# Rotating the queries of both head groups of a token tile in one set of vector operations, inside the loaded buffer

## The chip, the cores and the metric

The kernel runs on one core of a Trainium2 chip. The metric is the device time of one execution in microseconds (us): the median of three runs of the kernel before is 1649.61 us (1648.79 to 1650.91). Beside the times there is one profiled execution, with a record of each instruction on the engines: PE (TensorE, matmuls and transposes into PSUM), DVE (VectorE), ACT (ScalarE), POOL (GpSimd, unused here) and SP, whose queue issues all the DMAs.

## The reference

The kernel computes one encoder block on 1024 tokens of width 1024, in float32. A normalised input is projected into the inputs of two branches. Branch A is gated linear attention, branch B is softmax attention in a window of 128 tokens to both sides, with 8 query heads in 2 groups of 4 that share a key and value head. The branches are gated, summed and projected, and a SwiGLU feed-forward block follows. The part that matters here is the query side of branch B:

```python
q = _rope(_rms_norm(q.reshape(bsz, s, SWA_HEADS, hd), q_g), pos)
...
scores = jnp.einsum("bnqhgd,bnkhd->bnhgqk", qb, kc) * (hd ** -0.5)
...
m = jnp.maximum(scores.max(axis=-1, keepdims=True), sink)
p = jnp.exp(scores - m)
```

with `_rope` turning the two halves of a head's 128 values: `[x1*cos - x2*sin, x2*cos + x1*sin]`.

## The kernel before

Matmul operands are split into a high and a low part (`ACTIVATE Copy` on ACT writes the high part, a subtraction on DVE the low part), and a product is three matmuls. So nearly every matmul operand costs one ACT and one DVE instruction.

The program has these stages in time: the input and first projections; linear attention of branch A, with dense projections between its steps; softmax attention of branch B, with dense projections between its steps (about 384 to 578 us in the profile); the rest of the gate projections; output projections; and the feed-forward block.

Branch B works on 8 tiles of 128 tokens (t = 0 to 7) and 2 groups of heads (g = 0, 1). The list `todo` (L796 to L809) puts the steps of a tile and group into slots; a slot is one turn of a loop, and each step is a function that emits instructions:

- `prep(t)`, slot 2t+1: loads the 8 heads of queries of a tile from DRAM into `qr` (two DMAs, L665, buffer of 128 x 1024 values, two buffers), squares them on ACT (L666), loads keys and values of the next tile (L671), squares the keys (L672), sums the squares of each head on DVE (L674), takes an inverse root (L96 to L101) into `rs`, and rotates the next tile's keys (`rope_k`, L646 to L654).
- `a_rope(g, t)`, slot 2t+1 for g = 0 and 2t+2 for g = 1: four DVE operations on the 4 heads of a group. Two products with the sine table write the halves of `rq` (L699, L701), one with the cosine table writes a new tile `qn4` (L703), and a sum adds `rq` to it in place (L704). The query norm's gain is in the tables `qA` and `qB`; the inverse root `rs` is applied later, in the softmax.
- `a_turn(g, t)`, slot 2t+2+g: PE transposes the 4 heads (L710), ACT and DVE split them (L713, L714).
- `a_scores(g, t, h)`, four times, slot 2t+3+g: scores of a head (L727, through the helper `mm` at L73), added to the band and reduced to a maximum on DVE (L728); after the fourth head the softmax: small DVE operations, four exponentials (L743) and four scalings (L749) on ACT.
- `a_probs(g, t, kb)`, up to three times, slot 2t+4+g: PE transposes the probabilities of a block of keys (L760), ACT and DVE split them (`ph` at L763, `pl` at L764).
- `a_out(g, t)`, slot 2t+5+g: products with the values, copied by ACT (L774) and stored by four DMAs (L776).
- `k_turn(t)`, transposes of keys (L689), in even slots.

In a slot the steps are sorted by `order` (L810), and `slot` (L273) runs them one after the other and spreads a fixed number of dense matmuls evenly behind them (`share(SF, t)`: 24 in slots 2 to 8, 18 in slots 9 to 17). These dense matmuls (L245 and L73 with an `mm` bank) belong to the projections; their results go out by DVE (L248) and DMA (L251), and their weights are split by L67 and L69. Scores, transposes, probabilities and outputs share four PSUM banks (`ch`); a bank comes free when ACT or DVE has read it.

PE runs in the order in which the code is written (`manual_schedule`). The order of DVE's, ACT's and SP's instructions is chosen at build time by the framework's planner, from priorities in the order of the program and estimated times; on the chip each of these queues then runs strictly in that order, and waits at its head hold everything behind them. A buffer of a pool is handed on when all that read it are done.

Of the kernel before, what the change touches and what calls it, by code (L numbers as in the profile page):

```python
# [8 lines left out]
F32 = mybir.dt.float32  # L9
# [3 lines left out]
ALU = mybir.AluOpType  # L13

P = 128
# [15 lines left out]
def body(tc, i, out):  # L31
    nc = tc.nc
    with ExitStack() as root:
# [8 lines left out]
        def nm(s):  # L42
            uid[0] += 1
            return f"{s}_{uid[0]}"
# [49 lines left out]
        def rsqrt(dst, v, scale, epsv, eps_t, pool, shape, tag):  # L94
            l = pool.tile(list(shape), F32, tag=tag + "l", name=nm("rl"))
            nc.scalar.activation(l, v, AF.Ln, bias=eps_t[:, 0:1], scale=scale)  # L96
            nc.scalar.activation(l, l, AF.Exp, scale=-0.5)
            t = pool.tile(list(shape), F32, tag=tag + "t", name=nm("rt"))
            nc.vector.scalar_tensor_tensor(t, l, -0.5 * scale, l, op0=ALU.mult, op1=ALU.mult)
            nc.vector.scalar_tensor_tensor(t, v, epsv / scale, t, op0=ALU.add, op1=ALU.mult)  # L100
            nc.vector.scalar_tensor_tensor(dst, t, 1.5, l, op0=ALU.add, op1=ALU.mult)  # L101
# [167 lines left out]
        def need(key):  # L269
            while key not in scr:  # L270
                fill(12)
# [346 lines left out]
        sw = swas.enter_context(tc.tile_pool(name="swt", bufs=2))  # L618
# [7 lines left out]
        qA = sc_.tile([P, KT, P], F32, tag="qA", name="qA")  # L626
        qB = sc_.tile([P, KT, P], F32, tag="qB", name="qB")
# [12 lines left out]
        keys, att = {}, {}  # L640

        def rope_k(raw, rs, t):
            qn = sw.tile([P, 2, P], F32, tag="qn2", name=nm("qn"))
            b = sw.tile([P, 2, P], F32, tag="sq2", name=nm("sq"))
            for h in range(2):
                nc.vector.scalar_tensor_tensor(qn[:, h], raw[:, h], rs[:, h:h + 1], kg, op0=ALU.mult, op1=ALU.mult)  # L646
            c = cosb[:, t:t + 1].to_broadcast([P, 2, 64])
            s = sinb[:, t:t + 1].to_broadcast([P, 2, 64])
            nc.vector.tensor_tensor(b[:, :, 0:64], qn[:, :, 64:128], s, op=ALU.mult)
            nc.vector.tensor_tensor(b[:, :, 64:128], qn[:, :, 0:64], s, op=ALU.mult)  # L650
            nc.vector.tensor_tensor(qn[:, :, 0:64], qn[:, :, 0:64], c, op=ALU.mult)
            nc.vector.tensor_tensor(qn[:, :, 64:128], qn[:, :, 64:128], c, op=ALU.mult)
            nc.vector.tensor_tensor(qn[:, :, 0:64], qn[:, :, 0:64], b[:, :, 0:64], op=ALU.subtract)
            nc.vector.tensor_tensor(qn[:, :, 64:128], qn[:, :, 64:128], b[:, :, 64:128], op=ALU.add)  # L654
            return qn

        def prep(t):
            sq = sw.tile([P, 10, P], F32, tag="sq", name=nm("sq"), bufs=1)
            lo, hi = 8, 8
            if t >= 0:  # L660
                lo = 0
                qr = sw.tile([P, 8, P], F32, tag="qr", name=nm("qr"))
                for g in range(2):
                    need((f"sq{g}", t))
                    nc.sync.dma_start(out=qr[:, 4 * g:4 * g + 4].rearrange("p a b -> p (a b)"), in_=scr[f"sq{g}", t])  # L665
                nc.scalar.activation(sq[:, 0:8], qr, AF.Square)  # L666
            if t + 1 < KT:
                hi = 10
                kv = sw.tile([P, 4, P], F32, tag="kvr", name=nm("kvr"), bufs=1)
                need(("skv", t + 1))  # L670
                nc.sync.dma_start(out=kv.rearrange("p a b -> p (a b)"), in_=scr["skv", t + 1])  # L671
                nc.scalar.activation(sq[:, 8:10], kv[:, 0:2], AF.Square)  # L672
            ss = sw.tile([P, 10], F32, tag="ss", name=nm("ss"))
            nc.vector.tensor_reduce(ss[:, lo:hi], sq[:, lo:hi], axis=mybir.AxisListType.X, op=ALU.add)  # L674
            rs = sw.tile([P, 10], F32, tag="rs", name=nm("rs"), bufs=4)
            rsqrt(rs[:, lo:hi], ss[:, lo:hi], 1.0, EPS * 128, eps128, sw, (P, hi - lo), f"sn{hi - lo}")
            if t + 1 < KT:
                keys[t + 1] = rope_k(kv, rs[:, 8:10], t + 1)
                v2 = kv[:, 2:4].rearrange("p a b -> p (a b)")
                nc.scalar.activation(vSh[t + 1], v2, AF.Copy)  # L680
                nc.vector.tensor_tensor(vSl[t + 1], v2, vSh[t + 1].bitcast(F32), op=ALU.subtract)
            for g in range(2 if t >= 0 else 0):
                a = att[g, t] = Chunk()
                a.qr, a.rs = qr[:, 4 * g:4 * g + 4], rs[:, 4 * g:4 * g + 4]

        def k_turn(t):
            kt = chtile((P, 2, P))
# [3 lines left out]
            nc.scalar.activation(kTh[:, :, c], kt, AF.Copy)  # L691
            nc.vector.tensor_tensor(kTl[:, :, c], kt, kTh[:, :, c].bitcast(F32), op=ALU.subtract)

        def a_rope(g, n):
            a = att[g, n]
            qr = a.qr
            b = sw.tile([P, 4, P], F32, tag="rq", name=nm("rq"), bufs=1)
            a.qn = sw.tile([P, 4, P], F32, tag="qn4", name=nm("qn"))
            nc.vector.tensor_tensor(b[:, :, 0:64], qr[:, :, 64:128], qB[:, n:n + 1, 0:64].to_broadcast([P, 4, 64]),  # L699
                                    op=ALU.mult)  # L700
            nc.vector.tensor_tensor(b[:, :, 64:128], qr[:, :, 0:64], qB[:, n:n + 1, 64:128].to_broadcast([P, 4, 64]),  # L701
                                    op=ALU.mult)
            nc.vector.tensor_tensor(a.qn, qr, qA[:, n:n + 1].to_broadcast([P, 4, P]), op=ALU.mult)  # L703
            nc.vector.tensor_tensor(a.qn, a.qn, b, op=ALU.add)  # L704

        def a_turn(g, n):
            a = att[g, n]
# [87 lines left out]

        todo = [[] for _ in range(2 * KT + 6)]  # L796
        todo[0].append((prep, -1))
        todo[1].append((k_turn, 0))
        for n in range(2 * KT):
            t, g = divmod(n, 2)  # L800
            todo[n + 5].append((a_out, g, t))
            todo[n + 4] += [(a_probs, g, t, kb) for kb in range(3)]
            todo[n + 3] += [(a_scores, g, t, h) for h in range(4)]
            todo[n + 2].append((a_turn, g, t))
            todo[n + 1].append((a_rope, g, t))
            if g == 0:
                todo[n + 1].append((prep, t))
                if t + 1 < KT:
                    todo[n + 2].append((k_turn, t + 1))  # L809
        order = (prep, a_rope, a_scores, a_turn, k_turn, a_out, a_probs)  # L810
        with tc.manual_schedule(engines={mybir.EngineType.PE}):
            for t, v in enumerate(todo):
# [229 lines left out]
        def gate(nme, s):  # L1042
            g = bt.tile([P, HT], F32, tag=nme[:2], name=nm(nme[:2]))
            nc.sync.dma_start(out=g, in_=scr[nme, s])
            nc.scalar.activation(g, g, AF.Sigmoid)
            return g
# [119 lines left out]
        with tc.manual_schedule(engines={mybir.EngineType.PE}):  # L1166
# [29 lines left out]
            for m in (0, 4, 1, 5, 2, 6, 3, 7):  # L1196
                g = [gate(f"gb{m}", s) for s in range(2)]
# [345 lines left out]
```

## Time and profile before

| what | value |
|---|---|
| median of three runs | 1649.61 us |
| the profiled execution's own time | 1647.86 us |
| its span, first to last instruction | 1646.1 us |
| mean granted TensorE clock | 0.995 |
| PE busy | 1621.1 us (98%), 7644 matmuls and transposes |
| DVE busy | 1230.9 us (75%), 2358 instructions |
| ACT busy | 913.7 us (56%), 1867 instructions |
| `qr` loads (L665) | 16 |
| rotation of queries (L699, L701, L703, L704) | 16 instructions a line |

A line of the trace that begins with two numbers gives the start and the duration of an instruction in us, then engine, line of the kernel, operation, output and inputs by the program's names with the buffer numbers left out, and in square brackets the idle time of the engine before it and what ended it. A line of waits gives who waited for whom, the total in us, how many times, and the longest. Busy time is the share in which an engine ran anything; idle time of an engine that nobody waits for costs nothing.

### The profile page before, as it was taken

The numbers are of one execution on the slowest core, as the hardware profiler recorded it, in microseconds if no ns is written. First come the engines' busy times: TensorE is split into PE (matmuls) and PEld (weight loads), VectorE is DVE, ScalarE is ACT, GpSimd is POOL, SyncE is SP. The second block draws the span as 40 slices with busy tenths as digits, with TensorE's granted clock in tenths as the row PEclk, the third lists the DMA queues.
The fourth block names the chain that finished last, engine by engine and source line by source line (L and its number), as shares of the span: only waits on it lengthen the run. The fifth ranks groups of instructions, "written<-read, shape, count | busy, mean of one in ns | idle before, by whom it ended". The sixth has DMA issues, their size and how long they took to land.

```text
span 1646.1 us, 23402 instructions
## 1 busy us (share of the span) xinstructions
PE 1621.1 (98%) x7644; PEld 1346.5 (82%) x7644; DVE 1230.9 (75%) x2358; ACT 913.7 (56%) x1867; POOL 0.2 (0%) x4
## 2 busy tenths in 40 slices
PE   9999999999999999998999999999999999999999
PEld 7888888888888788886888888888888888788887
DVE  8568787846999677785865787776767787779655
ACT  7456776863988745453633546754444444354442
POOL 0000000000000000000000000000000000000000
PEclk9999999999999999998999999999999999999999
DMA  8856757778543387776842476643444555595433
GB/s 284 292 167 205 240 186 241 268 265 298 188 133 116 123 288 248 250 230 229 262 131 89 143 228 201 202 152 129 130 127 150 196 191 174 185 335 190 148 99 118
DMA packets 195787, 322.21 MB, mean 196 GB/s; under 512 B 22254, under 2 KB 47726, under 8 KB 195664
## 3 DMA queue, kind: packets, MB, share of 16 engines
q1 hardware_dynamic: 195664, 320.71, 59.4%
q8 instruction: 60, 0.98, 0.3%
q14 instruction: 63, 0.52, 0.1%
HBM read 215.24 MB, written 105.38 MB: 195 GB/s over the span
## 4 chain that ended last, share of the span: by engine, by line
PE 88%; DVE 5%; ACT 4%; DMA 2%; issue 1%; SPq 0%; ACTq 0%; DVEq 0%
PE mm L73 19%; PE mm L852 10%; PE mm L854 10%; PE mm L853 10%; PE mm L1383 7%; PE ch L73 7%; PE ch L1383 5%; PE ch L852 5%; PE ch L854 5%; PE ch L853 5%; PE mm L245 3%; PE ch L760 1%; ACT p L743 1%; DVE G L421 1%; DVE wl L69 0%
## 5 line engine op out<-in xcount | busy, mean ns | idle before, releaser
L831 ACT ACTIVATE wh<-ws 128x512 fp32r<-128x512 f32 x164 | 103.2, 630 | 155.2 <-PE mm L853 87.4
L73 PE MATMUL mm<-wh,xh 128*128 128x512 f32 x320 | 127.3, 398 | 0.1
L73 PE MATMUL mm<-wh,xl 128*128 128x512 f32 x320 | 127.1, 397 | 0.0
L73 PE MATMUL mm<-wl,xh 128*128 128x512 f32 x320 | 126.6, 396 | 0.0
L832 DVE TENSOR_TENSOR wl<-ws,wh 128x512 fp32r<-128x512 f32 x164 | 112.4, 686 | 15.8 <-ACT wh L831 15.1
L67 ACT ACTIVATE wh<-wr 128x512 fp32r<-128x512 f32 x118 | 73.8, 627 | 59.6 <-PE mm L73 25.8
L69 DVE TENSOR_TENSOR wl<-wr,wh 128x512 fp32r<-128x512 f32 x118 | 81.0, 688 | 22.6 <-ACT wh L67 20.0
L831 ACT ACTIVATE wh<-a 128x512 fp32r<-128x512 f32 x66 | 41.7, 632 | 91.0 <-PE ch L1383 42.3
L831 ACT ACTIVATE wh<-wr 128x512 fp32r<-128x512 f32 x72 | 45.4, 631 | 55.7 <-PE mm L853 16.9
L832 DVE TENSOR_TENSOR wl<-a,wh 128x512 fp32r<-128x512 f32 x66 | 45.6, 692 | 40.5 <-ACT wh L831 40.2
L1383 PE MATMUL mm<-hh,wh 128*128 128x512 f32 x176 | 68.6, 390 | 0.5 <-DVE c L1322 0.5
L1383 PE MATMUL mm<-hl,wh 128*128 128x512 f32 x176 | 68.6, 390 | 0.0
L1383 PE MATMUL mm<-hh,wl 128*128 128x512 f32 x176 | 68.5, 389 | 0.0
L73 PEld LDWEIGHTS mm<-wl,xh 128*128 128x128 f32 x320 | 60.2, 188 | 9.9
L73 PEld LDWEIGHTS mm<-wh,xl 128*128 128x128 f32 x320 | 60.2, 188 | 9.7
L73 PEld LDWEIGHTS mm<-wh,xh 128*128 128x128 f32 x320 | 60.2, 188 | 9.3 <-ACT st L220 0.3
L845 DVE TENSOR_TENSOR ws<-wr,wr 128x512 f32<-128x512 f32 x80 | 54.8, 688 | 6.3 <-DMA wr<-in_w_f_dram 3.6
L1356 DVE TENSOR_TENSOR hl<-hr,hh 128x512 fp32r<-128x512 f32 x77 | 52.9, 687 | 5.9 <-ACT hh L1355 5.7
L832 DVE TENSOR_TENSOR wl<-wr,wh 128x512 fp32r<-128x512 f32 x72 | 49.3, 686 | 5.6 <-ACT wh L831 4.7
L1355 ACT ACTIVATE hh<-hr 128x512 fp32r<-128x512 f32 x77 | 47.6, 619 | 8.8 <-DMA hr<-B 4.9
L1383 PE MATMUL ch<-hh,wh 128*128 128x512 f32 x132 | 51.3, 389 | 0.0
L1383 PE MATMUL ch<-hl,wh 128*128 128x512 f32 x132 | 51.3, 389 | 0.0
(453 smaller groups left out, 5008.4 us busy)
## 6 DMA issues: line engine op xcount, KB each, us to landing
wr<-in_w_fi_dram SPq DMA_DIRECT2D x110, 256.0 KB, 3.9
wr<-in_w_f_dram SPq DMA_DIRECT2D x100, 256.0 KB, 3.4
wh<-wh SPq DMA_DIRECT2D x80, 256.0 KB, 2.9
wl<-wl SPq DMA_DIRECT2D x80, 256.0 KB, 2.9
B<-c SPq DMA_DIRECT2D x44, 256.0 KB, 2.1
T<-st SPq DMA_DIRECT2D x44, 256.0 KB, 2.9
a<-in_w_fo_dram SPq DMA_DIRECT2D x44, 256.0 KB, 5.2
hr<-T SPq DMA_DIRECT2D x44, 256.0 KB, 2.6
```

The costliest lines, as they stand in the source:

```text
L67: nc.scalar.activation(h, raw, AF.Copy)
L69: nc.vector.tensor_tensor(l, raw, h.bitcast(F32), op=ALU.subtract)
L73: nc.tensor.matmul(o, a, b, start=start, stop=stop)
L245: nc.tensor.matmul(Y[q], w[:, c], x, start=f0, stop=f1, skip_group_check=True)
L831: nc.scalar.activation(h, src, AF.Copy)
L832: nc.vector.tensor_tensor(l, src, h.bitcast(F32), op=ALU.subtract)
L845: nc.vector.tensor_tensor(t, x, y, op=op)
L852: nc.tensor.matmul(o, h[:, c], x[kk][0], start=start and kk == 0, stop=False, skip_group_check=True)
L853: nc.tensor.matmul(o, h[:, c], x[kk][1], start=False, stop=False, skip_group_check=True)
L854: nc.tensor.matmul(o, l[:, c], x[kk][0], start=False, stop=kk == nk - 1, skip_group_check=True)
L1356: nc.vector.tensor_tensor(l, r, h.bitcast(F32), op=ALU.subtract)
L1383: nc.tensor.matmul(ys[m], a[:, c], b, start=f0, stop=f1, skip_group_check=True)
```

## The change

`a_rope` is called once for a token tile, in slot 2t+1, in place of once for each group in slots 2t+1 and 2t+2. Its operations take all 8 heads. The product with the cosine table and the sum write into `qr` itself, so the tile `qn4` (two buffers of 2 KB a partition) is gone, and `rq` has twice its size (4 KB a partition, one buffer). `a_turn` reads its 4 heads from `qr`. Even slots have one step less; the number of dense matmuls in a slot stays.

```diff
             for g in range(2 if t >= 0 else 0):
                 a = att[g, t] = Chunk()
-                a.qr, a.rs = qr[:, 4 * g:4 * g + 4], rs[:, 4 * g:4 * g + 4]
+                a.q8, a.qn, a.rs = qr, qr[:, 4 * g:4 * g + 4], rs[:, 4 * g:4 * g + 4]
...
-        def a_rope(g, n):
-            a = att[g, n]
-            qr = a.qr
-            b = sw.tile([P, 4, P], F32, tag="rq", name=nm("rq"), bufs=1)
-            a.qn = sw.tile([P, 4, P], F32, tag="qn4", name=nm("qn"))
-            nc.vector.tensor_tensor(b[:, :, 0:64], qr[:, :, 64:128], qB[:, n:n + 1, 0:64].to_broadcast([P, 4, 64]),
-                                    op=ALU.mult)
-            nc.vector.tensor_tensor(b[:, :, 64:128], qr[:, :, 0:64], qB[:, n:n + 1, 64:128].to_broadcast([P, 4, 64]),
-                                    op=ALU.mult)
-            nc.vector.tensor_tensor(a.qn, qr, qA[:, n:n + 1].to_broadcast([P, 4, P]), op=ALU.mult)
-            nc.vector.tensor_tensor(a.qn, a.qn, b, op=ALU.add)
+        def a_rope(n):
+            qr = att[0, n].q8
+            b = sw.tile([P, 8, P], F32, tag="rq", name=nm("rq"), bufs=1)
+            for d, o in ((0, 64), (64, 0)):
+                nc.vector.tensor_tensor(b[:, :, d:d + 64], qr[:, :, o:o + 64],
+                                        qB[:, n:n + 1, d:d + 64].to_broadcast([P, 8, 64]), op=ALU.mult)
+            nc.vector.tensor_tensor(qr, qr, qA[:, n:n + 1].to_broadcast([P, 8, P]), op=ALU.mult)
+            nc.vector.tensor_tensor(qr, qr, b, op=ALU.add)
...
-            todo[n + 1].append((a_rope, g, t))
             if g == 0:
-                todo[n + 1].append((prep, t))
+                todo[n + 1] += [(a_rope, t), (prep, t)]
```

## The prediction

> **What bounds the kernel now.** I read the page's first part, then the busy times of each engine by stretch over the attention stage (its work runs from about 384 to 578 us), then who waited for whom in it.
>
> ```profile
> span 1646.1 us, 23402 instructions
> PE 1621.1 (98%) x7644; PEld 1346.5 (82%) x7644; DVE 1230.9 (75%) x2358; ACT 913.7 (56%) x1867; POOL 0.2 (0%) x4
> ```
>
> ```profile
> 400.00:560.00 160.00, 156.60 (x847) 132.47 (x846) 146.35 (x450) 139.88 (x337) 0.00 (x0) 1.00 0.48 154
> 560.00:580.00 20.00, 17.47 (x79) 13.44 (x78) 9.28 (x26) 11.54 (x28) 0.00 (x0) 0.91 0.40 116
> ```
>
> TensorE sets the time: it is idle for 25.0 us of the whole span. Columns of the second view: stretch, its length, PE, PEld, DVE, ACT, POOL, granted clock, DMA. From 400 to 560 PE idles 3.4 us, in the last 20 us another 2.5 us, and there the granted clock averages 0.91, which loses up to 0.09 x 20 = 1.8 us. So all that this stage can give is 3.4 + 2.5 + 1.8 = 7.7 us. DVE has 13.7 us free in 160 and ACT 20.1: neither is the bound of the stage, but each is full enough that the order of its queue shows.
>
> ```profile
> PE ch L73 <- DVE pl L764: 1.5, 2, 0.8
> PE ch L73 <- DVE sql L714: 0.8, 1, 0.8
> PE ch L73 <- DVE mx L728: 0.6, 3, 0.2
> PE ch L73 <- DVE rd L747: 0.4, 1, 0.4
> ACT sq L666 <- DMA qr<-sq: 3.1, 3, 1.3
> SPq L251 <- DVE st L248: 28.2, 15, 6.5
> ```
>
> (Total, times, longest, 380 to 565 us.) What DVE costs PE here is 1.5 + 0.8 + 0.6 + 0.4 = 3.3 us. No rotation (L699 to L704) is waited for by PE; it only stands in DVE's queue ahead of what is.
>
> **Fewer, longer instructions.** Per token tile four pairs become four single operations of twice the width: 64 DVE instructions in eight tiles become 32.
>
> ```profile
> 384.27 0.42 DVE L699 TENSOR_TENSOR rq<-qr,qB 128x256 f32<-128x256 f32 x1
> 384.61 0.42 DVE L701 TENSOR_TENSOR rq<-qr,qB 128x256 f32<-128x256 f32 x1
> 384.94 1.29 DVE L703 TENSOR_TENSOR qn<-qr,qA 128x512 f32<-128x512 f32 x2
> 386.15 0.69 DVE L704 TENSOR_TENSOR qn<-qn,rq 128x512 f32<-128x512 f32 x1
> ```
>
> ```profile
> L674 DVE TENSOR_REDUCE ss<-sq 128x8 f32<-128x1024 f32 x1 | 1.2, 1220 | 0.0
> ```
>
> By durations a tile costs 2 x (2 x 0.42 + 2 x 0.69) = 4.44 us now and 2 x 0.69 + 2 x 1.22 = 3.82 after; the 1.22 is the row of another operation over 1024 elements, since no such multiply is in the trace. But starts lie closer than durations: 0.34 us apart at 256 elements, (386.15 - 384.94) / 2 = 0.605 at 512, so 0.605 + 2 x (0.605 - 0.34) = 1.135 at 1024. By starts a tile costs 3.78 us now and 3.48 after: 0.30 less, 2.4 us in eight tiles. I take the starts, for back to back is how they run. The in-place product is no extra cost: L704, in place already, lasts as long as half of the L703 pair. All of it lies beside PE's work; alone it is worth nothing, except through the order below.
>
> The Trainium skill ("VectorE: DVE Perf Modes", The DRAIN you can't avoid) says that the next operation does not start until the pipe is empty, and its rules for authors ask for fewer operations. By that the whole fixed part, 2 x 0.42 - 0.69 = 0.15 us, would be saved 32 times, 4.8 us of DVE. The rows differ: L701 starts 0.08 us before L699 ends.
>
> **The second group's rotation moves a slot earlier.** Slot 2t+2 loses it (1.89 us by starts), slot 2t+1 has 3.48 us in place of 1.89. This is where the odd slot of tile 5 has its wait:
>
> ```profile
> 482.28 1.48 DVE L674 TENSOR_REDUCE ss<-sq 128x10 f32<-128x1280 f32 x1
> 484.00 0.42 DVE L699 TENSOR_TENSOR rq<-qr,qB 128x256 f32<-128x256 f32 x1
> 485.79 0.69 DVE L703 TENSOR_TENSOR qn<-qr,qA 128x512 f32<-128x512 f32 x1
> 486.47 0.69 DVE L69 TENSOR_TENSOR wl<-wr,wh 128x512 fp32r<-128x512 f32 x1
> 487.16 1.85 DVE L764 TENSOR_TENSOR pl<-ch,ph 128x512 fp32r<-128x512 f32 x3
> 488.93 0.69 DVE L704 TENSOR_TENSOR qn<-qn,rq 128x512 f32<-128x512 f32 x1
> ```
>
> ```profile
> 486.17 1.54 ACT L763 ACTIVATE ph<-ch 128x512 fp32r<-128x512 f32 x3
> ```
>
> ```profile
> 487.96 0.41 PE L73 MATMUL ch<-kTh,sqh 128*128 128x384 f32 x1 [0.80 <-DVE pl L764]
> ```
>
> PE's second score waits 0.80 us for a PSUM bank that pl (L764) frees. The first ph ends near 486.75 (1.54 us hold three), so pl could start there and started at 487.16: DVE owns 0.41 of the wait, ACT the rest. Behind the changed rotation the three operations ahead of pl grow by 2 x 0.265 + 0.53 = 1.06 us, but the slot before has given up 1.89. If the free time is used, pl starts with ph: -0.41 us a tile. If the 1.135 us product stands right ahead of pl, as a 0.6 us operation does now: +0.53. For tiles 2 to 7 that is -2.5 to +3.2 us; the ends nearly cancel and I take 0.
>
> **The loaded queries are held longer.** qr has two buffers. Now the last read of a tile is L703 of group 1; after the change the rotated queries lie in qr, so its buffer comes free when PE has transposed group 1 (L710).
>
> ```profile
> 474.69 0.69 DVE L703 TENSOR_TENSOR qn<-qr,qA 128x512 f32<-128x512 f32 x1
> 504.41 1.48 DVE L674 TENSOR_REDUCE ss<-sq 128x10 f32<-128x1280 f32 x1
> ```
>
> ```profile
> 475.40 0.32 SPq L665 DMA_DIRECT2D qr<-sq  x1
> ```
>
> ```profile
> 490.76 0.60 PE L710 MATMUL ch<-ident,qn 128*128 128x128 f32 x4
> ```
>
> ```profile
> DMA to landing us min/median/max: 2.6/3.7/5.4
> ```
>
> ```profile
> 490.44 1.06 ACT L666 ACTIVATE sq<-qr 128x1024 f32<-128x1024 f32 x1
> 494.84 1.27 ACT L763 ACTIVATE ph<-ch 128x512 fp32r<-128x512 f32 x2 [0.31 <-PE ch L760]
> 504.25 0.59 ACT L774 COPY st<-ch 128x512 f32<-128x512 f32 x1 [0.75 <-PE ch L73]
> ```
>
> The load of tile 6 goes out at 475.40, as soon as L703 is done; it would go out at about 491.4, 16 us later, and land by 495.1 (497.2 with the longest landing). Its square (L666) then ends by 498.3 at best, and the sum that needs it ran at 504.41: 6 us remain, so the wait for data costs nothing. It is the place on ACT that changes: the square ran at 490.44; after the change it comes into the stretch from 494.84 on in which ACT idles next only for 0.75 us ahead of 504.25. Its 1.06 us push what follows by up to 1.06 - 0.75 = 0.31 us, and the chain ACT, ph, pl, PE is the one just shown. Four steady tiles: 0 to +1.2 us; I take a third, +0.4, since only some slots wait there at all. On SP the two loads now wait for PE; behind them stand the stores of results and the loads of dense weights. SP stood up to 6.5 us on a dense store without a wait of PE, so that is covered; uncovered, it would be part of the first rival. The product in place also waits for ACT's square: 498.3 against a rotation that starts after the sum, no cost.
>
> **The run-ahead at the start goes.** Tiles 2 and 3 are now prepared two slots ahead, and that has a price:
>
> ```profile
> 409.24 1.49 DVE L674 TENSOR_REDUCE ss<-sq 128x10 f32<-128x1280 f32 x1 [0.28 <-ACT sq L672]
> ```
>
> ```profile
> 399.80 0.99 SPq L665 DMA_DIRECT2D qr<-sq  x2
> ```
>
> ```profile
> 408.50 0.60 PE L710 MATMUL ch<-ident,qn 128*128 128x128 f32 x4
> ...
> 411.52 0.38 PE L73 MATMUL ch<-kTh,sql 128*128 128x256 f32 x1 [0.79 <-DVE sql L714]
> ```
>
> The sum of tile 2 stands ahead of sql, for which PE waits 0.79 us. Its load went out at 399.8 and could now go only after the transposes of tile 0's second group (L710 at 408.50), so the sum comes later and this wait may go: -0.8 to 0, I take -0.4.
>
> **PE's own order.** In the eight even slots one stage is gone, so the one or two dense matmuls that stood ahead of the first score come behind it.
>
> ```profile
> 496.67 0.39 PE L245 MATMUL mm<-xh,wl 128*128 128x512 f32 x1
> 496.90 0.34 PE L73 MATMUL ch<-kTh,sqh 128*128 128x384 f32 x1
> ```
>
> The first score of an even slot has no wait in the trace, and as many dense matmuls are issued in the slot as before: 0; bound +1.8 (eight times the 0.23 us from the dense matmul's start to the next).
>
> **Sum.** 0 + 0.4 - 0.4 + 0 = 0 on the span of 1646.1 us and on the profiled execution's 1647.86, which is 1.75 below the median of the timed runs. I forecast that median, 1649.6.
>
> **Rivals.** (1) Slower: ACT stands at the square. The queue of ACT is fixed at build time; if the square is put where its data are thought to be there, and the load behind PE and SP comes later, exponentials and ph of the running tile stand behind it. Three times ACT waited for qr already, 3.1 us, 1.03 each. For tiles 2 to 7 that is 6 x 1.03 = 6.2 us if all of it passes to PE: 1655.8. It decides as soon as the landing is later than ACT's slack of 0.75 us. For it: the load is now gated by PE for six tiles. Against: 6 us to the sum. Chance 0.19.
> The Trainium skill ("Perfetto Trace Analysis", Identifying Performance Opportunities) takes a gap that repeats on the saturated engine as a sign of too few buffers. Longer use of qr's two would make one a tile; the trace of before shows 0.80 at 487.96 but behind pl, not behind a load.
> (2) Faster: the freed 2.4 us and the early wait let DVE catch up, and all 3.3 us go: 1646.3, on the edge of what can be told. Against: half of the wait shown is ACT's. Chance 0.26.
> (3) The end of the stage shifts.
>
> ```profile
> 567.97 0.50 PE L73 MATMUL ch<-ph,vSh 128*128 128x512 f32 x1 [1.31 <-ACT ph L763]
> ```
>
> There PE waits and its clock falls: 2.5 + 1.8 = 4.3 us. No rotation is left there, yet another order of DVE before it could close it, 1645.3 (0.12), or double it, 1653.9 (0.08).
>
> **How the numbers follow.** Forecast 0.35; with its own bounds (-2.5 - 0.8 to +3.2 + 1.2 + 1.8) it reaches from 1646.3 to 1655.8, most of it within 1648 to 1652. Against no change 0.2%, 3.3 us, can be told. Faster: half of (2) and the closed end, 0.13 + 0.12 = 0.25. Slower: (1) and the doubled end, 0.27. Same: 0.48. The range 1645.0 to 1656.0 takes in every case's price.
>
> **What would show it.** Right: 32 DVE instructions fewer; the wide ones at 0.69 and 1.22 us; loads of qr right behind L710's last transpose; square after 495 us without a DMA wait on ACT; PE busy from 400 to 560 within 1 us of 156.6. Wrong: ACT idle on qr in several tiles, pl waits over 1.2 us in odd slots, or another PE idle time near 565 us.

## The result and the profile after

The changed kernel takes 1664.28 us (median of 6 runs, 1660.7 to 1665.73) against 1649.2 (6 runs beside them): a ratio of 1.0087, 95% interval 1.0074 to 1.0100, some 15 us slower. The forecast was 1649.6, with a range that ended at 1656.0. The profiled execution of the changed kernel took 1664.0 us.

The lines of the changed kernel lie a few lower than before: products into `rq` L698, the two operations in place L700 and L701, the transposes of the queries L707, the score evacuation L725, `ph` L760, `pl` L761. The first two lines of its page, and then its busy times by stretch (columns as in the prediction):

```profile
span 1662.2 us, 23387 instructions
PE 1628.2 (98%) x7644; PEld 1348.2 (81%) x7644; DVE 1229.1 (74%) x2326; ACT 915.0 (55%) x1867; POOL 0.2 (0%) x4
```

```profile
400.00:560.00 160.00, 147.43 (x760) 121.63 (x759) 136.72 (x391) 126.50 (x301) 0.00 (x0) 0.98 0.47 147
400.00:600.00 200.00, 184.94 (x939) 151.26 (x938) 158.98 (x453) 153.61 (x366) 0.00 (x0) 0.97 0.45 140
460.00:480.00 20.00, 16.73 (x81) 13.86 (x80) 16.19 (x47) 15.76 (x37) 0.00 (x0) 0.91 0.36 122
500.00:520.00 20.00, 18.47 (x94) 15.21 (x93) 17.96 (x51) 13.85 (x33) 0.00 (x0) 0.91 0.40 129
```

From 400 to 560 TensorE did 760 matmuls where it had done 847; it idles 12.6 us instead of 3.4, and in two stretches the granted clock averages 0.91, which was 1.00 there before. Up to 384 us both have run the same matmuls but one (2029 and 2028). The first matmul behind the stage, in the timelines of the kernel before and of the changed one, shows that all of the loss lies inside it:

```profile
595.27 0.39 PE L852 MATMUL ch<-xh,wh 128*128 128x512 f32 x1
```

```profile
613.13 0.39 PE L848 MATMUL ch<-xh,wh 128*128 128x512 f32 x1
```

It starts 17.9 us later, and from there to the end the two spans are 1050.8 and 1049.1 us. From 384 us to this matmul PE idles 15.4 us where it idled 5.9. The other 8.4 us of the delay are time in which PE is busy but gets the same work done more slowly. The clock has a part in it: it averages 0.83 from 470 to 480 and from 510 to 520 us, 0.79 from 580 to 590 and 0.87 from 590 to 600, where the kernel before has one such stretch (0.83 from 570 to 580).

The instructions themselves came out as the prediction had them. Groups of the changed kernel from 380 to 600 us, with total and mean ns:

```profile
L698 DVE TENSOR_TENSOR rq<-qr,qB 128x512 f32<-128x512 f32 x16 | 10.5, 683 | 5.4 <-DMA qr<-sq 5.4
L701 DVE TENSOR_TENSOR qr<-qr,rq 128x1024 f32<-128x1024 f32 x8 | 9.7, 1218 | 0.0
L700 DVE TENSOR_TENSOR qr<-qr,qA 128x1024 f32<-128x1024 f32 x8 | 9.7, 1217 | 0.1
```

What changed is who waits for whom. Waits of the changed kernel from 380 to 600 us (total, times, longest):

```profile
PE ch L73 <- DVE pl L761: 3.5, 5, 1.4
PE ch L707 <- DVE mx L725: 3.3, 1, 3.3
PE ch L73 <- DVE mx L725: 3.0, 5, 0.9
PE ch L73 <- ACT ph L760: 2.1, 2, 1.3
PE ch L73 <- DVE sql L711: 0.9, 1, 0.9
ACT sq L666 <- DMA qr<-sq: 6.6, 6, 2.8
DVE rq L698 <- DMA qr<-sq: 5.4, 3, 2.7
```

Before, PE's waits that end on the score evacuation were 0.6 us; now they are 6.3. ACT's waits for the loaded queries doubled from 3.1 us, and DVE's are 5.4 where they were 4.3, but PE waits for neither directly: it waits for PSUM banks that DVE empties late. The longest of these waits, as the timeline has it on DVE, on ACT, on PE and on the queue of SP:

```profile
455.87 1.29 DVE L698 TENSOR_TENSOR rq<-qr,qB 128x512 f32<-128x512 f32 x2 [0.58 <-DMA qr<-sq]
...
467.90 0.69 DVE L248 TENSOR_TENSOR st<-mm,rstd 128x512 f32<-128x512 f32 x1 [2.03 <-DMA b<-st]
468.62 1.89 DVE L761 TENSOR_TENSOR pl<-ch,ph 128x512 fp32r<-128x512 f32 x3
470.42 0.68 DVE L69 TENSOR_TENSOR wl<-wr,wh 128x512 fp32r<-128x512 f32 x1
471.05 1.23 DVE L700 TENSOR_TENSOR qr<-qr,qA 128x1024 f32<-128x1024 f32 x1
472.20 1.48 DVE L674 TENSOR_REDUCE ss<-sq 128x10 f32<-128x1280 f32 x1
473.59 0.41 DVE L681 TENSOR_TENSOR vSl<-kvr,vSh 128x256 fp32r<-128x256 f32 x1
473.93 1.22 DVE L701 TENSOR_TENSOR qr<-qr,rq 128x1024 f32<-128x1024 f32 x1
475.16 0.55 DVE L725 CUSTOM_DVE_ANT_0 p<-ch,band 128x384 f32<-128x384 f32 x1
```

```profile
469.96 1.05 ACT L666 ACTIVATE sq<-qr 128x1024 f32<-128x1024 f32 x1
479.85 1.06 ACT L666 ACTIVATE sq<-qr 128x1024 f32<-128x1024 f32 x1 [2.79 <-DMA qr<-sq]
```

```profile
468.86 0.34 PE L73 MATMUL ch<-kTh,sqh 128*128 128x384 f32 x1
472.11 0.39 PE L245 MATMUL mm<-xl,wh 128*128 128x512 f32 x1
475.77 0.66 PE L707 MATMUL ch<-ident,qr 128*128 128x128 f32 x4 [3.27 <-DVE mx L725]
477.33 0.63 PE L73 MATMUL ch<-pl,vSh 128*128 128x512 f32 x1
```

```profile
476.46 0.80 SPq L665 DMA_DIRECT2D qr<-sq  x2
```

Read from the bottom of the wait: PE computed the four heads' scores from 468.86 on and filled all four `ch` banks. The next step needs a bank, and the first evacuation (L725) ran only at 475.16. Ahead of it DVE had stood 2.03 us behind a store, then did three `pl`, a weight split, and from 471.05 to 475.07 the rotation with the sum of squares between its halves. The products into `rq` had run at 455.87; L700 may not run before the square, at 469.96 in ACT's queue, has read what it overwrites. It starts as that ends, but DVE, busy with the weight split until then, shows no wait for it: what can be seen is where L700 stands in the queue, not that the square held it up. The wait behind the store is new as well (5.9 us in two waits from 380 to 600 us, none before), and no run takes it away alone; a later kernel without any such wait, the one with the in-place operations halved, is still 11 us slower than the kernel before. Behind the gap the matmuls of 512 columns last 0.63 us instead of 0.39. And only now, with the transposes at 475.77, is the buffer free: the next load goes out at 476.46, so the lateness goes into the next tile, whose square makes ACT wait 2.79 us.

The Trainium skill ("TensorE: Matmul & The Clock Gate", Part 1: The HAM clock gate) says that TensorE falls to half its clock after an idle window of about 3.4 us. The trace agrees in kind, with a gap a little shorter than that: the 3.27 us are followed by the 0.63 us matmuls, and the granted clock averages 0.83 from 470 to 480 us.

### The profile page after: what moved, and what is told of

It reads as the page before. It is cut to its first block, busy times and chain, and to the rows that moved or that the text cites. A ratio compares the mean times of both kernels' runs of the same rounds, so it can differ in the third digit from the quotient of the medians.

```text
span 1662.2 us, 23387 instructions
## 1 busy us (share of the span) xinstructions
PE 1628.2 (98%) x7644; PEld 1348.2 (81%) x7644; DVE 1229.1 (74%) x2326; ACT 915.0 (55%) x1867; POOL 0.2 (0%) x4
## 4 chain that ended last, share of the span: by engine, by line
PE 81%; DVE 8%; ACT 5%; DMA 3%; issue 2%; SPq 1%; ACTq 0%; DVEq 0%
PE mm L73 16%; PE mm L848 10%; PE mm L850 10%; PE mm L849 10%; PE mm L1379 7%; PE ch L73 5%; PE ch L1379 5%; PE ch L849 5%; PE ch L850 5%; PE ch L848 5%; PE mm L245 2%; DMA qr<-sq 1%; ACT p L740 1%; DVE wl L69 1%; DVE G L421 1%
```

## The experiments

Four things changed at once: the second group's rotation moved a slot earlier, the loaded buffer is held until PE has read it ("held" below), the order of the operations within the step, and their width. Theory one was the held buffer: the late load turns the slack of ACT and DVE into waits. Rivals were PE's changed order, the move by itself, the length of the operations, and, once a control had shown it possible, the place of the tiles in SBUF. Medians stand beside those of the kernel before on the same chips, 1648.6 to 1649.2 us. The 95% intervals of the ratios reach some 1.5 to 3 us to each side, so two kernels that differ by less are not told apart.

**Single parts, on the kernel before.** PE's order alone, the rotation staying where it was (the even slot's first step emits it):

```diff
...
+                if t >= 2 and t % 2 == 0 and t // 2 - 1 < KT:
+                    fs[0] = lambda f=fs[0], m=t // 2 - 1: (a_rope(1, m), f())
...
```

> The kernel before with its rotations in their slots and their own tile, but the second group's rotation no step of its own in the even slots, so that the order of PE's instructions is exactly that of the changed kernel. Order on PE: 1658 us or more. Late load, or rotation moved: 1647 to 1652 us.

Measured: 1648.5 us, ratio 0.9999 (0.999 to 1.0009). PE's order costs nothing.

Both groups' rotations in the odd slot, four heads wide, into their own tiles:

```diff
+        def a_rope2(n):
+            for g in range(2):
+                a_rope(g, n)
...
-            todo[n + 1].append((a_rope, g, t))
...
+                todo[n + 1].append((a_rope2, t))
...
```

> The kernel before with both groups' rotations, still four heads wide and into their own tiles, as one step of the odd slot; the order of PE's instructions is exactly that of the changed kernel. Rotation moved: 1656 us or more with DVE-ended waits of PE over 6 us. Order on PE: 1658 us or more. Late load: the queries' buffer comes free even earlier than before, 1646 to 1652 us.

Measured: 1649.93, ratio 1.0006 (0.9996 to 1.0015). The move alone is not to be told from nothing.

The hold alone, in place but four wide and in the old slots:

```diff
-            a.qn = sw.tile([P, 4, P], F32, tag="qn4", name=nm("qn"))
+            a.qn = qr
```

> The kernel before, with its two rotations of four heads in their two slots and its order on PE, but the product and the sum written into the loaded queries in place of a tile of their own. Late load: the buffer is held as in the changed kernel, 1658 to 1668 us, ACT waits on the load 4 us or more. Rotation moved and widened, or order on PE: nothing of them is in it, 1647 to 1652 us.

Measured: 1653.94, ratio 1.0033 (1.002 to 1.0046): about 5 us, less than the 1658 to 1668 that theory one expected. Its waits from 380 to 600 us have a kind that the kernel before has not, DVE standing until ACT has squared what it is to overwrite:

```profile
ACT sq L666 <- DMA qr<-sq: 3.5, 5, 1.3
DVE qr L703 <- ACT sq L666: 2.0, 2, 1.5
```

Hold and move together, still four wide, are the two edits above in one:

> Both groups' rotations as one step of the odd slot, in place in the two buffers of loaded queries, but four heads wide: the changed kernel without the wide operations. The order of PE's instructions is the changed kernel's. Late load made worse by the move: 1659 to 1666 us, as the changed kernel. Width: it is gone, so 1653 to 1658 us, about the cost of the late load alone (1654).

Measured: 1652.55, ratio 1.0027 (1.0015 to 1.0039). This kernel has PE's order of the changed kernel, its late load and its operations in place, and still it is 11.7 us faster. Its ACT waited longer for queries than the changed kernel's (6.6 us), so that wait alone decides nothing:

```profile
ACT sq L666 <- DMA qr<-sq: 8.7, 5, 2.6
```

With three buffers of `qr` in it, which make the load early again:

> As the run before this one, with three buffers for the loaded queries: four heads wide, in the odd slot, in place, no late load. Width: it is gone and so is the late load, 1647 to 1651 us. Product in place: what was left with three buffers stays, 1653 to 1657 us.

Measured: 1651.18, ratio 1.0010 (1.0000 to 1.0020): 1.4 us back, which is less than the two intervals can tell from nothing.

**Taken from the changed kernel.** Three buffers in place of two:

```diff
-                qr = sw.tile([P, 8, P], F32, tag="qr", name=nm("qr"))
+                qr = sw.tile([P, 8, P], F32, tag="qr", name=nm("qr"), bufs=3)
```

> The changed kernel with three buffers for the loaded queries in place of two; the order of PE's instructions is the changed kernel's, and everything else is too. Late load (the load of tile t+2 now waits until PE has transposed tile t's second group, and ACT and DVE stand at it): the cause is gone, 1646 to 1652 us, ACT waits on the load under 2 us in all, PE busy 155 us or more from 400 to 560. Rotation moved and widened (3.5 us of DVE work at once in the odd slots): it stays, 1660 us or more. Order of the dense matmuls on PE: it stays, 1660 us or more.

Measured: 1654.41, ratio 1.0031 (1.0021 to 1.0042): 9.9 us of the 15 are back. PE's waits on the score evacuation fall from 6.3 us to 2.3, as its waits from 380 to 600 us show:

```profile
PE ch L73 <- DVE mx L725: 1.3, 5, 0.5
PE ch L707 <- DVE mx L725: 1.0, 1, 1.0
```

A tile of its own for the rotated queries, eight heads wide. For room the spare tile of the right-hand pools was shortened from 672 to 128 bytes:

```diff
-PAD = 672
+PAD = 128
...
-            nc.vector.tensor_tensor(qr, qr, qA[:, n:n + 1].to_broadcast([P, 8, P]), op=ALU.mult)
-            nc.vector.tensor_tensor(qr, qr, b, op=ALU.add)
+            qn = sw.tile([P, 8, P], F32, tag="qn8", name=nm("qn"))
+            nc.vector.tensor_tensor(qn, qr, qA[:, n:n + 1].to_broadcast([P, 8, P]), op=ALU.mult)
+            nc.vector.tensor_tensor(qn, qn, b, op=ALU.add)
...
```

> The changed kernel (one set of eight-head operations in the odd slot) with the product and the sum in a tile of their own of eight heads, two buffers, so that the loaded queries are free when the product has read them; room for it comes from 544 bytes less of unused space. The order of PE's instructions is the changed kernel's. Late load, or the product in place (which has to wait for ACT's square of the same data): both gone, 1647 to 1651 us. Width (a 1.2 us operation of DVE ahead of the operations that PE waits for): it stays as in the run with three buffers, 1653 to 1657 us.

Measured: 1662.16, ratio 1.0084 (1.0069 to 1.0100), outside of both forecasts. This seemed to speak against theory one, until the shift was tried by itself on the kernel before, with `PAD` as the only edit:

> The kernel before with 544 bytes less of unused space, nothing else: what the room taken in the run with the own tile does by itself. All theories: 1647 to 1651 us.

Measured: 1658.98, ratio 1.0067 (1.0052 to 1.0082). The order of instructions on every engine is the same as before; the addresses of the pools behind the spare tile alone cost 9.9 us. So the own tile has to be read against the changed kernel with the same shift:

> The changed kernel with its spare tile shortened from 672 to 128 bytes, so that the pools behind it lie 544 bytes lower; the order on every engine is unchanged. The kernel with its own eight-wide tile, which needed the same shift, took 1662.16. If holding the loaded buffer costs the most of it, this kernel is slower than that one by about 10 us: 1672 to 1675, the changed kernel's 1664.3 and the 9.9 that the shift cost the kernel before. If the own tile brought nothing, it comes to 1662 too, and the shift costs the changed kernel nothing.

Measured: 1674.76, ratio 1.0153 (1.0134 to 1.0173), as theory one had it. At the same addresses the own tile gives 12.6 us. The stretch from 400 to 600 us, first of the changed kernel so shifted, then with its own tile:

```profile
400.00:600.00 200.00, 185.37 (x940) 151.75 (x939) 157.37 (x451) 153.44 (x366) 0.00 (x0) 0.97 0.44 141
```

```profile
400.00:600.00 200.00, 192.12 (x994) 159.03 (x994) 166.27 (x467) 157.64 (x376) 0.00 (x0) 0.99 0.50 160
```

940 matmuls become 994, with operations as wide as the changed kernel's. Against the shifted kernel before (1658.98) the wide operations with a tile of their own cost some 3 us, about as much as the intervals can tell.

Addresses were then a rival for the 11.7 us too, since `rq` is larger in the changed kernel. The kernel with hold and move, with `rq` as large as there:

```diff
-            b = sw.tile([P, 4, P], F32, tag="rq", name=nm("rq"), bufs=1)
+            b = sw.tile([P, 8, P], F32, tag="rq", name=nm("rq"), bufs=1)[:, 0:4]
```

> The kernel with both rotations in the odd slot, four heads wide and in place, which took 1652.55 us, with one change: the tile rq is allocated at 4 KB a partition as in the changed kernel, and its first 2 KB are used. Instructions and their order on every engine are the same; only the SBUF addresses of the pool are those of the changed kernel. Theory 1 (the eleven further microseconds of the changed kernel come from the length of its vector operations): the time stays at 1652.5 within 1.5. Rival (they come from where the tiles lie in SBUF, as a shift by 544 bytes alone cost 9.9 us in the kernel before): 1660 or more. Anything between splits the eleven.

Measured: 1652.86, ratio 1.0024 (1.0015 to 1.0033). The room that `rq` takes has no part in it.

**Width, or place in the queue.** In the expectations of this part, theory 1 is no longer the held buffer but the length of the operations. The changed kernel with only the operations in place cut in halves of four heads:

```diff
-            nc.vector.tensor_tensor(qr, qr, qA[:, n:n + 1].to_broadcast([P, 8, P]), op=ALU.mult)
-            nc.vector.tensor_tensor(qr, qr, b, op=ALU.add)
+            for g in (slice(0, 4), slice(4, 8)):
+                nc.vector.tensor_tensor(qr[:, g], qr[:, g], qA[:, n:n + 1].to_broadcast([P, 4, P]), op=ALU.mult)
+                nc.vector.tensor_tensor(qr[:, g], qr[:, g], b[:, g], op=ALU.add)
```

> The changed kernel, with the product with the cosine table and the sum each cut into two halves of four heads (group 0's product and sum, then group 1's); the products into rq stay eight heads wide. No vector operation of the rotation is then longer than 0.69 us. Theory 1 (the 1.22 us operations, in place, stand ahead of score evacuations and of pl): 1652 to 1655, nearly all of the eleven microseconds gone, and PE's waits that end on the score evacuation back under 2 us between 380 and 600. Rival 1 (it is the eight-wide rq products that cost it): 1661 or more. Rival 2 (where the planner happens to put things differs from kernel to kernel by some microseconds, and the width decides little): anything from 1651 to 1664, with no order between this kernel and the next one.

Measured: 1659.8, ratio 1.0060 (1.0041 to 1.0078): 4.5 us back, less than expected. With only the products into `rq` cut, in the same way:

> The changed kernel, with only the two products into rq cut into halves of four heads (0.42 us each, four of them); the product with the cosine table and the sum stay eight heads wide, 1.22 us each. Theory 1 (the 1.22 us operations are the cause): stays between 1661 and 1666. Rival 1 (the rq products): 1652 to 1655. Rival 2 (the placement): anything from 1651 to 1664.

Measured: 1656.11, ratio 1.0040 (1.0025 to 1.0055): 8.2 us back, though both 1.22 us operations are still there. That the 1.22 us operations are the larger part falls with it; the rival's 1652 to 1655 is missed by 1 us. Both cuts together:

> The changed kernel with all four operations of the rotation in halves of four heads: first the four products into rq, then product and sum of group 0, product and sum of group 1. The work is that of the kernel with four-wide operations in place (1652.55), only the order within the one step differs. Theory 1 (the length of the operations costs it, 4.5 us by the in-place pair and 8.2 by the products, which add up): 1651 to 1654. Rival (it is luck of the order that the planner gives, and the two single cuts only happened to fall so): somewhere else, 1655 or more.

Measured: 1658.32, ratio 1.0058 (1.0041 to 1.0075). Nothing of the rotation is wide any more, the work is that of the kernel with hold and move, and it is still 5.8 us slower than that one. The lengths do not add up; the order does part of it. It is not the order in the program alone: written group after group, the second group's products must also wait until the first group has freed the one `rq` buffer, which keeps the groups apart. The timelines show how, here of the rotation of tile 5 on DVE, first where the step is written group after group (hold and move):

```profile
489.14 0.68 DVE L703 TENSOR_TENSOR qr<-qr,qA 128x512 f32<-128x512 f32 x1
...
490.52 1.85 DVE L768 TENSOR_TENSOR pl<-ch,ph 128x512 fp32r<-128x512 f32 x3
492.30 0.68 DVE L704 TENSOR_TENSOR qr<-qr,rq 128x512 f32<-128x512 f32 x1
492.89 0.55 DVE L732 CUSTOM_DVE_ANT_0 p<-ch,band 128x384 f32<-128x384 f32 x1
...
495.10 0.68 DVE L703 TENSOR_TENSOR qr<-qr,qA 128x512 f32<-128x512 f32 x1
```

and where all four products come first, with PE's wait behind it in a second view:

```profile
495.34 1.28 DVE L702 TENSOR_TENSOR qr<-qr,qA 128x512 f32<-128x512 f32 x2
496.54 1.28 DVE L703 TENSOR_TENSOR qr<-qr,rq 128x512 f32<-128x512 f32 x2
497.75 0.55 DVE L727 CUSTOM_DVE_ANT_0 p<-ch,band 128x384 f32<-128x384 f32 x1
```

```profile
498.36 0.66 PE L709 MATMUL ch<-ident,qr 128*128 128x128 f32 x4 [2.35 <-DVE mx L727]
```

In the first, `pl` and a score evacuation lie between the short operations. In the second, the four in-place ones run back to back from 495.34 to 497.75, ahead of every score evacuation of the step, and PE waits 2.35 us. Over the stage (380 to 600 us), first with hold and move, then with all products first, PE's waits on the score evacuation go from 2.1 to 6.4 us:

```profile
PE ch L764 <- DVE mx L732: 1.4, 2, 0.7
PE ch L73 <- DVE mx L732: 0.7, 1, 0.7
```

```profile
PE ch L73 <- DVE mx L727: 4.1, 6, 2.2
PE ch L709 <- DVE mx L727: 2.3, 1, 2.3
```

So one thing that matters is how much of the rotation stands as one block ahead of what PE waits for: a wide operation is such a block, and four short ones in a row are one too. It is not all that matters. These waits are 6.3 us in the changed kernel too, which is 6.0 us slower than this one. And with only the products cut they are 5.6 us and with only the in-place operations cut 3.2, though the first of these kernels is the faster.

Last, the changed kernel's whole rotation, wide and in place, one slot later:

```diff
-                todo[n + 1] += [(a_rope, t), (prep, t)]
+                todo[n + 1].append((prep, t))
+                todo[n + 2].append((a_rope, t))
```

> The changed kernel with the whole rotation, eight wide and in place, moved from the odd slot of a tile to the even slot behind it, ahead of the transposes that need it. The load is still gated by the transposes of the second group, and the operations are as long. Theory 1 (the held buffer together with the long operations): still slow, 1658 or more. Rival (the odd slot is a bad place for the lump, and the even slot would take it as it took group 1's rotation before): 1649 to 1654.

Measured: 1655.61, ratio 1.0044 (1.0029 to 1.0059): 8.7 us back, between what the theory and the rival expected. The same operations cost less where they fall elsewhere.

**What follows.** One path from the kernel before to the changed one, each step one edit more:

| kernel | us | step | PE idle, 384 to 615 us |
|---|---|---|---|
| before | 1649.2 | | 5.9 |
| both rotations in the odd slot | 1649.93 | 0.7 | 7.6 |
| in place, buffer held | 1652.55 | 2.6 | 9.9 |
| all products first, then the operations in place | 1658.32 | 5.8 | 13.2 |
| eight heads wide | 1664.28 | 6.0 | 15.4 |

PE's idle time in the stage, whatever ended it, grows along with the time (the last column is from the one profile of each kernel). The last step adds 2.2 us of it and two stretches of low clock, 0.83 from 470 to 480 and from 510 to 520 us, where the kernel of the step before has 1.00; by these figures the two stretches cost some 3.4 us (an estimate: 0.17 x 10 us, twice).

The steps hold along this path only: the hold by itself cost 5 us, and cutting one kind of operation gave 4.5 or 8.2. Each of three remedies takes away most of the loss: a third buffer 9.9, a tile of its own 12.6, a later slot 8.7. So it is no sum of prices. With the load early the wide operations cost little (some 5 us are left with the third buffer, some 3 with the tile of its own, which also spares the rotation the wait for ACT's square); with short operations spread through the queue the hold costs little; together they are dear. Each remedy also changes the planner's order: with the third buffer 311 of the 2326 DVE instructions stand at another place of the queue than in the changed kernel, so what the early load gives on its own is not shown. How the last 6.0 us divide between width and the queue order that the planner makes of it stays open: no edit here changed the width and left the order of DVE's queue as it was. No version beat the kernel before by more than the noise.

## Why the prediction was wrong

- **The operations.** Right: 2326 DVE instructions instead of 2358, durations of 0.68 and 1.22 us, and DVE's busy time fell by 1.8 us where 2.4 was estimated. That this is worth nothing alone was not tried by itself.
- **PE's own order.** Right: 0, confirmed by itself (1648.5).
- **The run-ahead at the start.** Wrong, and small: -0.4 was taken because the early wait for `sql` would go. It stayed: PE waits 0.9 us for it instead of 0.79.
- **The second group a slot earlier.** Right for the four-wide operations that the bounds were made from: 1649.93, no change. Wrong for the changed operations. The step costed 1.06 us of extra DVE work ahead of `pl` and took the free time of the slot as its cover. But the rotation did not keep its place: at 471 us it stands ahead of score evacuations, a wait that the step did not look at (0.6 us before, 6.3 after). Width alone does not explain this: the four short operations in a row have 6.4.
- **The held buffer.** This is the step that failed: "6 us remain, so the wait for data costs nothing", and for the product in place "no cost". The load does go out right behind PE's transposes, as forecast (476.46 behind 475.77). Two things were missed. The queues of ACT and DVE are ordered at build time, and the square and the products into `rq` often stand where the load has not landed yet, not where their results are needed: six of the eight squares wait, 6.6 us where ACT had waited 3.1, and DVE waits 5.4 us where it had waited 4.3. And the product in place cannot run before ACT's square. The step took it to run behind the sum of squares; in the wait shown it runs ahead of the sum (471.05 and 472.20), 15 us behind the products, and is part of the block that PE waited for. The slack was reckoned for one load in the old timeline, but now a late PE makes a late load, and a late load can make a late DVE and so a late PE. That loop has no term in the sum; the hold costs 5 us by itself, and without it the changed kernel is 9.9 to 12.6 us faster. (The 497.2 us of the step's longest landing is also a slip, 491.4 and 5.4 make 496.8, without effect.)
- **The rivals.** The first (ACT stands at the square) had the right sign and half of the mechanism, and its price of 6.2 us came near to the narrow forms (1652.6 to 1653.9 against 1655.8). It went wrong on the path: ACT's waits are not what passes to PE. The kernel with the longer wait of ACT, 8.7 us, is the faster one. Its chance of 0.19 was too low, and its price left out the clock, which averages 0.91 in the two stretches shown. The second rival did not happen. Of the third a part did: the waits on ACT at the end of the stage are 2.1 us as before, but by the prediction's own way of estimating the clock loses (0.21 + 0.13) x 10 = 3.4 us there, from 580 to 600, instead of 1.8.
- **The sum.** All terms were taken as independent. The runs show that hold, block and place make each other dearer, and no bound of a single term covered that. How the last 6.0 us, behind the step to wide operations, arise stays open.

## What to carry to other kernels

Before an operation is made to write into the buffer it reads, list everything that still reads this buffer and everything that waits for its release: here the square on ACT and the next load came to depend on PE's progress, and the saving of 2 us of DVE cost 15 us of the whole. Fewer and longer operations saved DVE time here and lost the whole, because something urgent stood behind them in a queue with a fixed order; look for the evacuations that would, and count the longest block ahead of them. When short operations are merged, try them written group after group as well: here that form, short operations included, was 5.8 us faster than the same short operations with all products first.

## What the runs showed of the hardware

A shift of SBUF addresses alone cost 9.9 us. Shifting by 544 bytes gave 1658.98, so a shift by 512 was tried, with `PAD = 160` as the only edit and again the same order on every engine:

> The kernel before with its spare tile shortened by 512 bytes, where the earlier run shortened it by 544 and lost 9.9 us with the same order on every engine. If the loss comes with any move of these pools: 1658 to 1660. If it comes with the odd 32 bytes: 1649, as before. This concerns how the kernels that needed the shift are to be compared, not the change itself.

Measured: 1648.36, ratio 0.9999 (0.999 to 1.0008). So it is not any shift that costs; two shifts do not show which ones do. Late in the program, from 1400 to 1600 us, the same group of matmuls of the kernel before and of the one shifted by 544 bytes:

```profile
L1383 PE MATMUL mm<-hh,wh 128*128 128x512 f32 x132 | 51.5, 390 | 0.5 <-DVE c L1322 0.5
```

```profile
L1383 PE MATMUL mm<-hh,wh 128*128 128x512 f32 x132 | 52.1, 394 | 0.1
```

The matmuls themselves are slower by 1% here, with no more waiting beside them and the granted clock at 1.00 in both; from 800 to 1400 us the two kernels run equally many (2652). Why the offset matters was not tried.

The granted clock also fell without a long gap. From 505 to 510 us of the changed kernel the waits of PE are 0.89 and 0.64 us, and the first matmul of 512 columns behind them lasts 0.63 us (the clock averages 0.83 from 510 to 520), though no gap comes near to the window that the page of the Trainium skill cited above names:

```profile
508.20 0.44 PE L73 MATMUL ch<-kTh,sqh 128*128 128x384 f32 x1 [0.89 <-DVE mx L725]
510.10 0.42 PE L73 MATMUL ch<-kTh,sqh 128*128 128x384 f32 x1 [0.64 <-DVE rd L744]
510.74 0.63 PE L245 MATMUL mm<-xh,wl 128*128 128x512 f32 x1
```
